# Experts in turn from the four groups, a further block's two halves in banks of their own, and bias products with 128 rows, in a hybrid backbone layer with a mixture of experts

## The chip, the cores and the metric

The kernel runs on one core of one Trainium2 chip. The metric is device time in microseconds (us), from the start of the program to its end, so lower is better. Before the change the median of 3 runs is 3455.18 us (3452.33 to 3460.63).

## What is computed

The reference is one layer: a token mix in two branches (a bidirectional recurrence with a matrix state per head, and a gated linear recurrence with a convolution), then a routed mixture of experts, each with a residual and a layer norm. Sizes: 1024 latent tokens, 256 context tokens, width 1024. Two pieces matter here. The first gives the recurrence its decays and its in-context rates, through low-rank ("lora") products of rank 64 with a bias, for both directions:

```python
w_log = -softplus(-(w0[:, None, None, :] + einsum('blr,erd->ebld', tanh(wd), w2))) - 0.5
decay = exp(-exp(w_log))
a = sigmoid(a0[:, None, None, :] + einsum('blr,erd->ebld', ad, a2))
```

The second is the mixture. There are 32 experts in 4 groups of 8. A token takes the best group, and in it the best two experts; an expert computes, for its tokens,

```python
(silu(xb @ w1[e]) * (xb @ w3[e])) @ w2[e]       # 1024 -> 512 -> 1024
```

## The kernel before, in words

The work goes through four parts one after the other: the input products and the linear recurrence (to some 940 us of the profile), the bidirectional recurrence (`phase_b`, to some 2340 us), the output products and the router (to some 2650 us), and the experts (`phase_d`, to some 3380 us), with a last layer norm behind them.

**The recurrence.** `phase_b` walks over 40 steps (4 pairs of heads' tiles, 10 pieces of 128 tokens), and for each over both directions `e`. The order of its instructions on every engine is written by a scheduler when the program is built, from generators that yield estimated delays; nobody wrote it by hand, so a small edit can move many rows. `stage_e` (L746) makes the decays and rates of one step and direction: four tiles of 128x128 in one PSUM bank, and for each of them four products that add up: three with 128 rows (L769 to L771, weights and inputs split into high and low bf16 parts) and one (L772) that adds the bias: its weights `T.b` are the bias in three bf16 parts, so 3 rows, and its moving operand is `ones3`, 3 rows of ones. ScalarE then takes the bank (L774). `T.b` is loaded once for each pair of tiles (L738), into a tile of 3 partitions.

**The experts.** `feed_weights` loads the weights: `todo` (L1283) lists, for each expert in the order of its number, 4 tiles of `e_w13` and 2 of `e_w2`, each of 1 MB; 16 such tiles fit on the chip. `ahead` (L1292) issues the next loads on SP's queue as tiles are given back. The tokens of an expert are gathered by an indirect DMA (`gather`), and transposed by TensorE (`x_t`).

Every expert has a first block of 64 tokens: `first` (L1688) computes its hidden values by `up` (L1619: 8 x 2 products of 512 columns, two half-height outputs side by side), `gate` (L1627) is silu on ScalarE and a multiplication on VectorE, `turn` (L1631) transposes on TensorE and copies on VectorE, `down` (L1638) multiplies with `e_w2`, and `put` (L1646) scales on VectorE and scatters the rows to memory from GpSimd. The loop at L1699 runs them interleaved: `first` of expert e+1, then `turn`, `x_t` and `down` around expert e. An expert with more than 64 tokens needs further blocks: `further` (L1671) loads the count into a register on every engine and branches; inside, `ffn` (L1658) is one further block. Up to three stand in nested branches. `ffn` has one PSUM bank `phb` for both halves of the hidden values (256 columns each), and runs them in turn:

```python
up(e, x, ph, A0)
gate(h, ph, A0)
up(e, x, ph, A1)
gate(h, ph, A1)
turn(hT, h, A0)
down(e, py, hT, A0)
turn(hT, h, A1)
down(e, py, hT, A1)
put(py, ap)
```

In `phase_d` the order on every engine is the order of the code (`manual_schedule`). PSUM there is full: two banks `ph` for the first blocks, one `phb`, one `pht`, two `py`, two for `x_t`. The counts of this input are such that 18 further blocks run: 11 in experts 8 to 15, 7 in experts 16 to 23, and none in experts 0 to 7 and 24 to 31.

## Time and profile before

| | |
|---|---|
| median of 3 runs | 3455.18 us (3452.33 to 3460.63) |
| the profiled execution, its own time | 3447.87 us |
| its span, first to last instruction | 3446.1 us |
| TensorE (PE) busy | 3091.9 us, 90% |
| VectorE (DVE) busy | 2162.2 us, 63% |
| ScalarE (ACT) busy | 1516.7 us, 44% |
| GpSimd (POOL) busy | 1231.1 us, 36% |
| mean granted TensorE clock | 0.921 of 2.4 GHz |

A row of the timeline gives the start, the duration, the engine, the line, output and inputs, the shapes and the count of merged instructions, and in brackets the idle time of the engine before it and what ended that. Matmuls overlap each other, and their ends are modelled: what a product costs in a stream is the distance from its start to the start of the next. A float32 product stands as two records.

### The profile page before, as it was taken

What the parts mean: (1) busy time and instruction counts of PE and PEld (TensorE: products, weight loads), DVE (VectorE), ACT (ScalarE), POOL (GpSimd) and SP (SyncE); (2) the same over time, 40 slices, a digit from 0 to 9 for tenths busy, and PEclk for the clock granted to TensorE, in tenths of its full rate; (3) what the DMA queues carried; (4) which work ended last, traced back from release to release, by engine and by line L of the source; (5) the groups of instructions that cost most, each with busy time, mean ns of one, the idle gap of its engine ahead of it and who ended that gap; (6) DMA issues with size and microseconds to landing.
All of it is one profiled execution on the core that took longest, in us unless ns stands there. A gap on an engine that the chain in (4) does not pass through costs nothing. (4 is left out here: it accounts for less than half of the span.)

```text
span 3446.1 us, 67028 instructions
## 1 busy us (share of the span) xinstructions
PE 3091.9 (90%) x26407; PEld 2288.7 (66%) x26407; DVE 2162.2 (63%) x4153; ACT 1516.7 (44%) x3127; POOL 1231.1 (36%) x1517
## 2 busy tenths in 40 slices
PE   7999998999999999999999999998886888988881
PEld 4877776777777878788878887886674333434330
DVE  6768998966638877987777878776585111111115
ACT  4466555667426666666566657653210000000003
POOL 1022322344325544755554557432042111111114
PEclk9999999999986999999878989999997999999996
DMA  5433345432532111311221123106426976484895
GB/s 207 136 109 107 128 140 187 140 98 80 174 132 60 55 57 52 98 51 58 66 78 46 54 65 95 39 16 202 153 93 253 407 280 254 168 321 177 336 380 213
DMA packets 265476, 496.80 MB, mean 144 GB/s; under 512 B 34690, under 2 KB 188002, under 8 KB 239484
## 3 DMA queue, kind: packets, MB, share of 16 engines
q1 hardware_dynamic: 243804, 443.16, 36.7%
q0 software_dynamic: 21280, 48.28, 3.8%
q8 instruction: 263, 4.31, 0.5%
q14 instruction: 129, 1.06, 0.1%
HBM read 437.37 MB, written 83.83 MB: 151 GB/s over the span
## 5 line engine op out<-in xcount | busy, mean ns | idle before, releaser
L234 PE MATMUL zl<-h_hi,wlo 128*128 128x512 f32 x944 | 326.5, 400 | 17.5 <-DVE wlo L157 17.5
L230 PE MATMUL zl<-h_hi,whi 128*128 128x512 f32 x944 | 325.7, 401 | 3.9 <-ACT acc L408 3.0
L232 PE MATMUL zl<-h_lo,whi 128*128 128x512 f32 x944 | 326.4, 400 | 0.6 <-DVE rstd L287 0.5
L1624 PE MATMUL ph<-r,xT 128*64 128x512 f32 x1024 | 254.1, 652 | 65.5 <-PEq L1674 33.7
L1649 POOL DMA_INDIRECT scr_yx<-yo,sidx x50 | 50.8, 1017 | 554.4 <-DVE yo L1648 235.5
L1613 ACT ACTIVATE xT<-pxt 128x512 f32<-128x512 f32 x37 | 22.1, 597 | 500.0 <-DVE hT L1636 423.4
L1624 PEld LDWEIGHTS ph<-r,xT 128*64 128x64 f32 x1024 | 90.6, 149 | 227.2 <-issue 224.8
L234 PEld LDWEIGHTS zl<-h_hi,wlo 128*128 128x128 f32 x944 | 179.6, 191 | 55.1 <-DVE wlo L157 20.0
L836 PE MATMUL pg<-qr,bk 64*128 64x128 f32 (+1 forms) x1280 | 211.3, 309 | 4.8 <-DVE bk L797 2.5
L230 PEld LDWEIGHTS zl<-h_hi,whi 128*128 128x128 f32 x944 | 179.6, 191 | 43.5 <-ACT acc L408 3.7
L232 PEld LDWEIGHTS zl<-h_lo,whi 128*128 128x128 f32 x944 | 180.4, 191 | 38.0 <-issue 1.4
L1636 DVE COPY hT<-pht 128x256 f32<-128x256 f32 x32 | 13.6, 425 | 299.0 <-PE pht L1635 299.0
L841 POOL TENSOR_TENSOR r<-st,hm 64x256 f32<-64x256 f32 x160 | 117.7, 736 | 212.7 <-ACT hm L840 208.9
L836 PEld LDWEIGHTS pg<-qr,bk 64*128 64x128 f32 x1280 | 176.6, 209 | 18.4 <-issue 4.8
L411 DVE SCALAR_TENSOR_TENSOR acc<-zt,drv,acc 128x960 f32<-128x960 f32 (+3 forms) x142 | 170.8, 1209 | 9.5 <-ACT acc L408 5.9
L1002 POOL TENSOR_TENSOR sp<-rv,pc 64x128 f32<-64x128 f32 x304 | 132.5, 454 | 93.7 <-DVE rv L1025 81.7
L893 PE MATMUL pu<-u,n 128*128 128x64 bf16 x2240 | 155.8, 200 | 3.8 <-DVE n L903 2.6
L157 DVE TENSOR_TENSOR wlo<-wraw,whi 128x1024 fp32r<-128x1024 f32 x67 | 101.1, 1509 | 86.9 <-ACT whi L156 83.1
L915 ACT ACTIVATE u<-pu 128x256 bf16<-128x256 f32 x280 | 106.0, 381 | 93.5 <-PE pu L893 89.5
L1624 PE MATMUL phb<-r,xT 128*64 128x256 f32 x1152 | 131.6, 381 | 14.2 <-DVE hb L1629 12.7
L893 PEld LDWEIGHTS <-n 128*128 128x128 bf16 x2240 | 124.0, 102 | 27.6 <-issue 7.8
L917 DVE TENSOR_TENSOR u<-pu,u 128x256 bf16<-128x256 f32 x280 | 115.7, 417 | 41.8 <-PE pu L893 38.1
(456 smaller groups left out, 8429.0 us busy)
## 6 DMA issues: line engine op xcount, KB each, us to landing
r<-in_e_w_dram SPq DMA_DIRECT2D x192, 1024.0 KB
wraw<-in_w_in_dram SPq DMA_DIRECT2D x59, 512.0 KB
adr<-in_w_ada_dram SPq DMA_DIRECT2D x32, 512.0 KB
zk<-scr_zk SPq DMA_DIRECT2D x80, 128.0 KB
kk<-scr_kk SPq DMA_DIRECT2D x80, 128.0 KB
lp<-scr_lp SPq DMA_DIRECT2D x80, 128.0 KB
v<-scr_zv SPq DMA_DIRECT2D x80, 128.0 KB
wada<-in_w_ada_dram SPq DMA_DIRECT2D x8, 1024.0 KB
```

Of the source, the lines that this page charges most:

```text
L157: nc.vector.tensor_sub(lo, raw, hi.bitcast(F32))
L230: nc.tensor.matmul(pz, z.hi[:, k], h_hi[:, k, t0:t0 + n], start=(k == 0), stop=False)
L232: nc.tensor.matmul(pz, z.hi[:, k], h_lo[:, k, t0:t0 + n], start=False, stop=False)
L234: nc.tensor.matmul(pz, z.lo[:, k], h_hi[:, k, t0:t0 + n], start=False, stop=(k == KT - 1))
L411: nc.vector.scalar_tensor_tensor(o, i, mures[:n, r, j:j + 1], o, op0=OP.mult, op1=OP.add)
L836: nc.tensor.matmul(pg[:, j, cols], G.bk[sr, e, j, 64 * h:64 * h + 128], G.qr[sr, e, j, cols], start=True, stop=True)
L841: G_.tensor_tensor(r[sr], w[sr], hm[sr], op=OP.subtract)
L893: nc.tensor.matmul(pt[:, j], l[:, j], r_ if len(r_.shape) == 2 else r_[:, j], start=first, stop=True, **kw)
L915: A_.activation(u, pt, AF.Copy)
L917: V.tensor_tensor(u, pt, u8, op=OP.add)
L1002: G_.tensor_tensor(sp[sr, e], G.rv[sr, h, e, :, i], pcs[:, e, :, k:k + 1].to_broadcast([64, 2, C]), op=OP.mult)
L1624: nc.tensor.matmul(ph[HALF[h]].rearrange("p a b c -> p (a b c)")[:, c], x[:, k], w13(e, k)[:, h, c], start=(k == 0), stop=(k == KT - 1))
```

## The change

1. **Bias products.** `ones3` and the bias weights become tiles of 128 rows, zeros but for the first three; the bias tile `lb` is one tile for the whole part, and each pair's load writes its first three rows.
2. **Experts' order.** `ORDER` takes one expert of each of the four groups in turn: 0, 8, 16, 24, 1, 9, ... Loads, gathers and the loop follow it; `q` is the place in the order, `e` the expert.
3. **Further blocks.** `ffn` takes two banks `pa` and `pb` from the ring `ph` that the first blocks use, `pht` gets a second bank, and `up` and `down` can run in pieces, with the transposes between the pieces.

```diff
-    ones3 = pk.tile([3, P], BF16, name="ones3")
-    V.tensor_scalar(ones3, ident[0:3], 0.0, 1.0, op0=OP.mult, op1=OP.add)
+    ones3 = pk.tile([P, P], BF16, name="ones3")
+    V.memset(ones3, 0.0)
+    V.tensor_scalar(ones3[0:3], ident[0:3], 0.0, 1.0, op0=OP.mult, op1=OP.add)
+    lb = pk.tile([P, 2, 2, 2, P], BF16, name="lb")
+    V.memset(lb, 0.0)
...
-        T.b = pe.tile([3, 2, 2, 2, P], BF16, name=f"b{pr}", tag="b")
-        nc.sync.dma_start(T.b.rearrange("p e i a c -> p e i (a c)"),
+        T.b = lb
+        nc.sync.dma_start(lb[0:3].rearrange("p e i a c -> p e i (a c)"),
...
-    todo = [(e, i) for e in range(NE) for i in range(6)]
+    todo = [(e, i) for e in ORDER for i in range(6)]
...
+ORDER = [8 * g + i for i in range(8) for g in range(4)]
...
-        pt = psx.tile([P, 2, P], F32, name="pht", tag="pht")
+        pt = psx.tile([P, 2, P], F32, name="pht", tag="pht", bufs=2)
...
-    acc_h = lambda nm: psx.tile([P, 2, 2, P], F32, name=nm, tag=nm, bufs=2 if nm == "ph" else 1)
+    acc_h = lambda: psx.tile([P, 2, 2, P], F32, name="ph", tag="ph", bufs=2)
...
-        ph, py, h, hT = acc_h("phb"), acc_y(), hidden("hb"), hidden("hbT")
-        up(e, x, ph, A0)
-        gate(h, ph, A0)
-        up(e, x, ph, A1)
-        gate(h, ph, A1)
+        pa, pb, py, h, hT = acc_h(), acc_h(), acc_y(), hidden("hb"), hidden("hbT")
+        up(e, x, pa, A0)
+        gate(h, pa, A0)
+        up(e, x, pb, A1, range(4))
         turn(hT, h, A0)
-        down(e, py, hT, A0)
+        up(e, x, pb, A1, range(4, KT))
+        gate(h, pb, A1)
+        down(e, py, hT, A0, (0,))
         turn(hT, h, A1)
+        down(e, py, hT, A0, (1,))
         down(e, py, hT, A1)
         put(py, ap)
...
-        for e in range(NE):
-            if e + 3 < NE:
-                gather(xgs[0][(e + 3) % 2], gidx[:, 0, e + 3:e + 4])
...
+        for q, e in enumerate(ORDER):
+            fetch(0, q + 3)
+            fetch(1, q + 2)
```

What moves on TensorE in a further block, first before (the rows of one `ffn`, behind the branch of L1674; `r_0` to `r_3` are the `e_w13` tiles, `r_4` and `r_5` the `e_w2` tiles):

```order
L1674 COMPARE_AND_BRANCH
L1624 MATMUL phb<-r_0_34562,xT 64x256 x4
L1624 MATMUL phb<-r_1_34564,xT 64x256 x4
L1624 MATMUL phb<-r_2_34566,xT 64x256 x4
L1624 MATMUL phb<-r_3_34568,xT 64x256 x4
...
L1635 MATMUL pht<-ident,hb 128x128
L1644 MATMUL py<-r_4_34570,hbT 64x512 x4
L1635 MATMUL pht<-ident,hb 128x128
L1644 MATMUL py<-r_5_34572,hbT 64x512 x4
```

and of the changed kernel, from the second half of the hidden values on (its lines are up to 7 higher: the branch is L1681, `up` L1628, `turn` L1639, `down` L1648):

```order
L1628 MATMUL ph<-r_0_34561,xT 64x256 x4
L1628 MATMUL ph<-r_1_34563,xT 64x256 x4
L1639 MATMUL pht<-ident,hb 128x128
L1628 MATMUL ph<-r_2_34565,xT 64x256 x4
L1628 MATMUL ph<-r_3_34567,xT 64x256 x4
L1648 MATMUL py<-r_4_34569,hbT 64x512 x2
L1639 MATMUL pht<-ident,hb 128x128
L1648 MATMUL py<-r_4_34569,hbT 64x512 x2
L1648 MATMUL py<-r_5_34571,hbT 64x512 x4
```

Before, both transposes stood behind all products of the hidden values and directly ahead of the products that need them. Now the first stands in the middle of the second half's products, and the second between two parts of the first half's `down`.

On VectorE the same block had the two multiplications of `gate`, then the two copies of `turn`; now they alternate:

```order
L1633 TENSOR_TENSOR hb<-ph,hb 128x128
L1640 COPY hbT<-pht 128x128
L1633 TENSOR_TENSOR hb<-ph,hb 128x128
L1640 COPY hbT<-pht 128x128
L1652 TENSOR_TENSOR yo<-py,gt_33547 128x512
```

In the recurrence the kinds and numbers of instructions on each engine stay the same but for two memsets on VectorE, and the order of TensorE's rows is the same for the first 193 of them behind the last output product; from there on the scheduler has written another order on every engine, with local exchanges throughout. The first place on TensorE, before and now:

```order
L769 MATMUL pl<-lp,w_6652 128x128
L770 MATMUL pl<-lp,w_6652 128x128
L771 MATMUL pl<-lp,w_6652 128x128
L772 MATMUL pl<-ones_6584,b_6654 128x128
L836 MATMUL pg<-qr_7302,bk_6656 128x64 x4
```

```order
L772 MATMUL pl<-lp,w_6655 128x128
L773 MATMUL pl<-lp,w_6655 128x128
L774 MATMUL pl<-lp,w_6655 128x128
L775 MATMUL pl<-ones_6584,lb 128x128
L839 MATMUL pg<-qr_7304,bk_6658 128x64 x4
```

The group of four stands as it stood; its bias product reads `lb` in place of `b`.

## Rows read from the trace of the kernel before

**Rows 1.** Windows of the recurrence and of a run of light experts.

```profile
core 0: us, PE busy (x) PEld busy (x) DVE busy (x) ACT busy (x) POOL busy (x), PEclk, DMA share, GB/s
1000.00:2300.00 1300.00, 1263.01 (x16894) 1054.28 (x16894) 1032.25 (x2671) 813.53 (x2193) 717.71 (x1120) 0.89 0.21 61
2700.00:2800.00 100.00, 80.78 (x354) 31.22 (x352) 12.84 (x24) 5.23 (x12) 18.29 (x18) 0.91 1.01 408
```

**Rows 2.** Timeline of PE in the recurrence at the full clock.

```profile
1507.20 0.23 PE L769 MATMUL pl<-lp,w 128*128 128x128 bf16 x1
1507.27 0.22 PE L770 MATMUL pl<-lp,w 128*128 128x128 bf16 x1
1507.32 0.22 PE L771 MATMUL pl<-lp,w 128*128 128x128 bf16 x1
1507.47 0.22 PE L772 MATMUL pl<-ones,b 3*128 3x128 bf16 x1
1507.63 0.23 PE L769 MATMUL pl<-lp,w 128*128 128x128 bf16 x1
```

**Rows 3.** Timeline of PE at half the clock.

```profile
1016.96 0.29 PE L769 MATMUL pl<-lp,w 128*128 128x128 bf16 x1
...
1017.61 1.96 PE L836 MATMUL pg<-qr,bk 64*128 64x64 f32 x8
```

**Rows 4.** Lines L771 and L772: duration ns min/median/max, first and last start.

```profile
L771 PE MATMUL pl<-lp,w x320: 216/219/314, 938.0 to 2254.8; 128*128 128x128 bf16 x160
L772 PE MATMUL pl<-ones,b x320: 224/224/284, 945.5 to 2255.0; 3*128 3x128 bf16 x160
```

**Rows 5.** Windows where the recurrence begins; columns as in group 1.

```profile
1012.80:1016.10 3.30, 2.55 (x25) 1.55 (x24) 1.82 (x3) 1.31 (x3) 2.38 (x6) 1.00 0.16 50
1016.10:1019.50 3.40, 3.40 (x19) 2.54 (x17) 0.86 (x2) 1.75 (x5) 2.66 (x6) 0.50 0.87 273
```

**Rows 6.** Waits of PE in the recurrence: us in total, times, longest.

```profile
PE pu L911 <- DVE u L917: 4.4, 5, 2.0
```

**Rows 7.** Timeline of PE, one further block.

```profile
2935.67 3.67 PE L1624 MATMUL phb<-r,xT 128*64 128x256 f32 x32 [0.70 <-DVE hb L1629]
2939.27 0.33 PE L1635 MATMUL pht<-ident,hb 128*128 128x128 f32 x1
2940.24 1.94 PE L1644 MATMUL py<-r,hbT 128*64 128x512 f32 x8 [0.64 <-DVE hbT L1636]
2942.82 1.94 PE L1644 MATMUL py<-r,hbT 128*64 128x512 f32 x8 [0.38 <-DVE hbT L1636]
```

**Rows 8.** Waits of PE among the experts.

```profile
PE py L1644 <- DVE hbT L1636: 18.5, 36, 0.6
PE phb L1624 <- DVE hb L1629: 12.7, 18, 0.7
```

**Rows 9.** Timeline of POOL: the scatters that begin and end a run.

```profile
2677.82 1.02 POOL L1649 DMA_INDIRECT scr_yx<-yo,sidx  x1 [10.98 <-DVEq L1674]
2808.27 1.03 POOL L1649 DMA_INDIRECT scr_yx<-yo,sidx  x1 [10.94 <-DVE yo L1648]
```

**Rows 10.** Timeline of PE, experts without further blocks.

```profile
2679.46 7.09 PE L1624 MATMUL ph<-r,xT 128*64 128x512 f32 x32 [2.67 <-PEq L1674]
2687.72 3.65 PE L1644 MATMUL py<-r,hT 128*64 128x512 f32 x16
2694.51 8.78 PE L1624 MATMUL ph<-r,xT 128*64 128x512 f32 x32 [3.13 <-PEq L1674]
...
2891.36 7.09 PE L1624 MATMUL ph<-r,xT 128*64 128x512 f32 x32 [2.22 <-PEq L1674]
...
3358.65 7.09 PE L1624 MATMUL ph<-r,xT 128*64 128x512 f32 x32 [0.48 <-PEq L1674]
```

**Rows 11.** Line L1674, the branch, on two engines: duration ns min/median/max.

```profile
L1674 PEldq COMPARE_BRANCH  x32: 70/5562/6924, 2661.1 to 3367.1; - x32
L1674 DVEq COMPARE_BRANCH  x32: 43/56/72, 2666.8 to 3370.7; - x32
```

More of the change, by code (lines that the diff above doesn't have):

```diff
@@ L1617, in w13, with up @@
         return RAW[e, k // 2].rearrange("p (k h c) -> p k h c", k=2, h=2)[:, k % 2]
-    def up(e, x, ph, parts):
+    def up(e, x, ph, parts, ks=range(KT)):
         c = slice(256 * parts.start, 256 * parts.stop)
-        for k in range(KT):
+        for k in ks:
             for h in range(2):
@@ L1636, in turn, with down @@
         V.tensor_copy(hT[:, parts], pt[:, parts])
-    def down(e, py, hT, parts):
+    def down(e, py, hT, parts, hs=range(2)):
         for i in range(parts.start, parts.stop):
             w = RAW[e, 4 + i].rearrange("p (h d c) -> p h d c", h=2, d=2)
-            for h in range(2):
+            for h in hs:
                 for d in range(2):
@@ L1654, in phase_d, with further @@
     hidden = lambda nm: bp.tile([P, 2, P], F32, name=nm, tag=nm, bufs=2)
-    acc_h = lambda nm: psx.tile([P, 2, 2, P], F32, name=nm, tag=nm, bufs=2 if nm == "ph" else 1)
+    acc_h = lambda: psx.tile([P, 2, 2, P], F32, name="ph", tag="ph", bufs=2)
     acc_y = lambda: psx.tile([P, 512], F32, name="py", tag="py", bufs=2)
     def ffn(e, x, ap):
-        ph, py, h, hT = acc_h("phb"), acc_y(), hidden("hb"), hidden("hbT")
-        up(e, x, ph, A0)
-        gate(h, ph, A0)
-        up(e, x, ph, A1)
-        gate(h, ph, A1)
+        pa, pb, py, h, hT = acc_h(), acc_h(), acc_y(), hidden("hb"), hidden("hbT")
+        up(e, x, pa, A0)
+        gate(h, pa, A0)
+        up(e, x, pb, A1, range(4))
         turn(hT, h, A0)
-        down(e, py, hT, A0)
+        up(e, x, pb, A1, range(4, KT))
+        gate(h, pb, A1)
+        down(e, py, hT, A0, (0,))
         turn(hT, h, A1)
+        down(e, py, hT, A0, (1,))
         down(e, py, hT, A1)
         put(py, ap)
-    def further(e, xT):
+    def further(q, xT):
+        e = ORDER[q]
         n = count(cnt[0:1, e:e + 1])
@@ L1676, in further @@
             with tc.If(n > 128):
-                x2 = x_t(xgs[1][e % 2], "xT2")
+                x2 = x_t(xgs[1][q % 2], "xT2")
                 ffn(e, x2[:, :, HALF[0]], sidx[:, 2, e:e + 1])
@@ L1680, in further, with fetch, first @@
                     ffn(e, x2[:, :, HALF[1]], sidx[:, 3, e:e + 1])
-    for e in range(2):
+    def fetch(b, q):
+        if q < NE:
+            gather(xgs[b][q % 2], gidx[:, b, ORDER[q]:ORDER[q] + 1])
+    for q in range(2):
         for b in range(2):
-            gather(xgs[b][e], gidx[:, b, e:e + 1])
+            fetch(b, q)
     with tc.manual_schedule():
         X, HID = {}, {}
-        def first(e):
-            HID[e] = acc_h("ph"), hidden("h")
-            up(e, X[e][:, :, HALF[0]], HID[e][0], AB)
+        def first(q):
+            HID[q] = acc_h(), hidden("h")
+            up(ORDER[q], X[q][:, :, HALF[0]], HID[q][0], AB)
         X[0] = x_t(xgs[0][0], "xT")
-        gather(xgs[0][0], gidx[:, 0, 2:3])
+        fetch(0, 2)
         first(0)
@@ L1698, in phase_d @@
         ahead(4)
-        for e in range(NE):
-            if e + 3 < NE:
-                gather(xgs[0][(e + 3) % 2], gidx[:, 0, e + 3:e + 4])
-            if e + 2 < NE:
-                gather(xgs[1][e % 2], gidx[:, 1, e + 2:e + 3])
-            if e + 1 < NE:
-                first(e + 1)
-            h, hT, py = HID[e][1], hidden("hT"), acc_y()
+        for q, e in enumerate(ORDER):
+            fetch(0, q + 3)
+            fetch(1, q + 2)
+            if q + 1 < NE:
+                first(q + 1)
+            h, hT, py = HID[q][1], hidden("hT"), acc_y()
             turn(hT, h, AB)
-            if e + 2 < NE:
-                X[e + 2] = x_t(xgs[0][e % 2], "xT")
-            if e + 1 < NE:
-                gate(HID[e + 1][1], HID[e + 1][0], AB)
+            if q + 2 < NE:
+                X[q + 2] = x_t(xgs[0][q % 2], "xT")
+            if q + 1 < NE:
+                gate(HID[q + 1][1], HID[q + 1][0], AB)
             down(e, py, hT, AB)
@@ L1714, in phase_d @@
             ahead(2)
-            if e + 1 < NE:
-                further(e + 1, X[e + 1])
+            if q + 1 < NE:
+                further(q + 1, X[q + 1])
                 ahead(4)
@@ L1742, in phase_d @@
             tt(po, S.io[:, None, :].to_broadcast([P, 16, P]), pb[:, :, None].to_broadcast([P, 16, P]), op=OP.is_equal)
-            px = psx.tile([P, 2, NE], F32, name="pxall", tag="pht")
+            px = psx.tile([P, 2, NE], F32, name="pxall", tag="pxt1")
             for j in range(16):
```

## The prediction, made blind

> **What bounds the kernel now.** I read the page first, for the busy shares, then windows over the two parts that the change touches, then the timeline of TensorE (PE) and its waits in each, because an average over the whole span says nothing on either part. In the recurrence [rows 1] PE is busy for 1263 of 1300 us, VectorE for 1032 (79%), and the longest group of PE's own waits is 4.4 us in all [rows 6]: this part is as long as PE's list of products, and what shortens the list shortens it. Matmuls overlap there, so the price of a product is the distance between starts, not its duration. The mean granted clock is 0.89. PE has two levels, 1.2 and 2.4 GHz, so about 2 x 0.11 x 1300 = 286 us of the part run at half the clock.
>
> Among the experts there are two different stretches. With further blocks, PE works without a pause except inside each block [rows 7]. Where experts have none ("light" ones: 0 to 8 and 22 to 31, with 11, 15 and 16), the DMA engines are full (share 1.01, 408 GB/s [rows 1]) and PE waits for 2.2 to 3.2 us ahead of the next expert's first product [rows 10]. The trace names PE's own sequencer at the branch of `further`, not a load. That branch takes PE 5.56 us in the median, while VectorE passes the same one in 0.056 us [rows 11]. A light expert takes 16.3 us: scatters of experts 0 and 8 start at 2677.82 and 2808.27 [rows 9], and 130.45 / 8 = 16.3.
>
> **The change, part by part.** The sum is made against the profiled execution's own 3447.87 us (span 3446.1). The median of the runs is 3455.18, 7.3 us more, so the forecast is put on the median.
>
> **Bias products.** In [rows 2] the 128-row products follow each other by 0.07 and 0.05 us, but the 3-row product starts 0.15 us behind its predecessor, and the next 128-row product 0.16 us behind it. With 128 rows it should stand in the stream like the others: 0.15 - 0.05 and 0.16 - 0.07 are 0.19 us, and 320 such products [rows 4] make 61 us of PE's time. The group of four takes 0.43 us now (1507.20 to 1507.63) and should take about 0.24. No row shows the saving on the part's length. The lower bound is 0: VectorE would be at 1032 of 1239 us, 83%, and could become what PE waits for. The upper bound adds the clock. A group takes 0.65 us at half the clock [rows 3], against 0.43, so each us at half loses 1 - 0.43 / 0.65 = 0.34 us, and 286 us lose 97. Where the part begins, the granted clock is 1.00 while PE runs almost nothing but these groups, with 2.55 us busy in 3.30, and 0.50 right behind them [rows 5]. If full rows kept a third of such stretches at 2.4 GHz, 32 us more would go: 93. A loss is possible too, since the scheduler writes another order; that is a rival below. I take 45, three quarters of 61, nearest to the row of PE's waits: they are so small that most of PE's saving should arrive, but a new order and a shorter list will uncover some waits. VectorE's two memsets and the once-allocated bias tile cost nothing: they run while output products fill PE, and the loads of the next pair wait for the last reader as before. If that cover were gone, it would be a fraction of a us, once.
>
> The Trainium skill has a rule against this term: "TensorE: Matmul & The Clock Gate", section "Why this matters for your kernels", says that one product with 32 rows takes the same time as one with 128. By it the 45 would be 0. Our durations agree with it (224 against 219 ns [rows 4]), the starts do not (0.15 and 0.16 against 0.05 and 0.07 us [rows 2]). The skill's "TensorEngine Tiling (Array Packing)", section "Key Properties", says that a change of tiling mode drains the engine, which fits the starts.
>
> **Further blocks.** In [rows 7] PE stands idle three times a block: 0.70 us ahead of the second half's products, which wait for `gate` of the first half since both write one bank; 0.64 us for the first copy of the transposed half; and 0.38 us for the second copy. That is 1.72 us, and 18 blocks make 31; the groups of waits say the same, 18.5 + 12.7 = 31.2 [rows 8]. In the new order each wait has cover. The second half's products go to another bank and start at once. `gate` of the first half (0.70) and the copy behind the first transpose (0.33 + 0.64) each lie beside half of those products, 3.67 / 2 = 1.83 us. `gate` of the second half (0.70) and the second copy (0.33 + 0.38) each lie beside a quarter of `down`, 1.94 / 2 = 0.97. The thinnest cover is 0.97 against 0.71; if the last one failed, 18 x 0.38 = 7 would come back. Bounds 24 and 31; I take 31, since every wait has its row and every cover is longer.
>
> The shared ring `ph` adds one wait: the first product of the next expert now needs ScalarE and VectorE to have passed the branch of the expert before, too, or its `gate` inside. Behind it on PE stands the whole next expert. In a light expert, VectorE is done when the scatter starts, 2677.82 [rows 9], and PE's product starts at 2679.46 [rows 10], so 1.6 us hide it, and this costs 0. Only where PE's own branch is short (0.48 us at 3358.65 [rows 10]) could a few tenths show, a few times: under 2 us, left at 0.
>
> **Order of the experts.** The runs of light experts are broken up: five at the start (0, 8, 16, 24, 1), at most three between heavy ones, six at the end. It is tempting to count the whole idle time of those runs as waiting for weights. But PE's own work in a light expert is 11.91 us (2679.46 to 2687.72 + 3.65), and the wait at the branch is 2.22 us at 2891.36 too [rows 10], right behind heavy experts where the loads had caught up. So 14.1 us remain, and 15.8 when the clock drops in the gap (products 8.78 instead of 7.09 us). In the mean that is 15.0, against 16.3: 1.3 us at best for each expert that leaves a run. Six light experts now come first behind a heavy one, three did before, and second ones gain in part: I take 7 us. Bounds are 0 (every light expert still pays branch and clock) and 15 x 1.3 = 20. The gathers and loads only change their order; POOL and SP issue as many as before.
>
> The Trainium skill speaks against a larger term: "Runtime: NRT & Kernel Launch", section "Instruction fetch mechanics", says that a taken branch whose target is not in the window forces a fetch of the target page before anything runs. By it this wait belongs to the branch, no order of the experts removes it, and the 7 would be near 0; the long branch on PE alone [rows 11] fits.
>
> Sum: 45 + 31 + 7 = 83. That gives 3447.87 - 83 = 3365 for an execution like the profiled one, and 3455 - 83 = **3372 us** for the median.
>
> **The rivals.**
>
> *PE's saving in the recurrence is given back.* The 3-row product costs the stream what any product costs, or VectorE and ScalarE take over. Against it stand the starts in [rows 2]; for it VectorE's 79%. Then 31 + 7 = 38 remain: 3417.
>
> *More than the forecast.* All 61 arrive, the clock keeps 32, the light experts give 20: 61 + 32 + 31 + 20 = 144, so 3311. [Rows 5] speak for the clock, but other groups of products also stand ahead of half-clock stretches, and the recurrence's waits are not zero.
>
> *Slower: the clock in the recurrence.* The new order there puts short products and waits together so that the clock is granted less. Place: 1000 to 2300 us. Price: 0.34 us for each us more at half. It eats the whole gain from 83 / 0.34 = 244 us more at half, a granted mean of 0.80 in place of 0.89. At 0.75 it would be 364 us more and 124 us lost: 3496. For it: such a stretch at 0.50 exists where waits and few products coincide [rows 5]. Against it: the same products are there, and what leaves them is idle time between starts.
>
> *The change doesn't do what it says* in the blocks: if the shared ring made `pa` or `pb` wait for a bank, the 31 would go and 3403 remain; the order of the rows gives each bank's last reader long before its next writer, so I leave this inside the forecast's range.
>
> **How the numbers follow.** Forecast 0.70, with a range of its own of 3335 to 3405; saving given back 0.13; more 0.10; clock 0.05; other 0.02. The range 3320 to 3420 takes in the forecast, nearly all of the first rival and a part of the second; below it I leave some 0.07, above it some 0.08. A difference of 0.2%, about 7 us, is what a measurement of this kernel can tell from none. Faster 0.91 (forecast, first and second rival, less a little for their edges), same 0.03, slower 0.06.
>
> **What would show it.** Right: the bias product starts 0.05 to 0.07 us behind its predecessor; the stretch between the first and the last group of four is shorter by about 45 us, at a granted clock of 0.89 or more; a further block has no bracketed wait on VectorE and takes 1.7 us less; PE's waits at the branch are still 2 to 3 us, some 20 times; DMA shares of 1.01 become rare. Wrong: starts of 0.15 us that stay (first rival); starts that shrink and a part that does not, with PE waiting for VectorE; a granted mean under 0.85 (third rival); or a wait of `ph` for VectorE ahead of an expert's first product.

## The result, and the profile after

The changed kernel takes 3418.95 us in the median of 20 runs (3389.43 to 3449.67), the kernel before 3457.20 in 20 runs beside it (3443.14 to 3497.36). The ratio is 0.9869, with a 95% interval of 0.984 to 0.9898: between 35 and 55 us faster. The profiled execution took 3421.91 us, with a span of 3420.1 and a mean granted clock of 0.913. The gain was forecast as 83 us and is about half of that. The forecast time of 3372 is missed by 47 us; 3418.95 lies inside the range by 1 us, less than the measurement can tell.

The window of the recurrence of [rows 1], now, and the whole recurrence, from the first `pl` to the last `pgf`, of the kernel before and then of this one:

```profile
core 0: us, PE busy (x) PEld busy (x) DVE busy (x) ACT busy (x) POOL busy (x), PEclk, DMA share, GB/s
1000.00:2300.00 1300.00, 1224.67 (x16798) 1063.03 (x16797) 1043.53 (x2656) 811.85 (x2186) 724.19 (x1116) 0.87 0.21 62
...
937.90:2340.50 1402.60, 1360.26 (x17801) 1134.82 (x17801) 1077.16 (x2761) 845.40 (x2262) 733.39 (x1144) 0.90 0.22 65
...
943.10:2342.50 1399.40, 1318.34 (x17736) 1141.30 (x17736) 1090.81 (x2753) 845.09 (x2260) 737.75 (x1140) 0.88 0.22 65
```

PE is busy for 38 us less of the same 1300 us, and the granted clock is lower. Over the whole recurrence PE is busy for 42 us less, and idle for 81.1 us where it was idle for 42.3. The line of its last products, L893 before, begins its last `pgf` at 2340.5 in the profile before and at 2342.5 now; from the first `pl` it is 1402.6 us before (937.9 to 2340.5) and 1399.4 now (943.1 to 2342.5).

```profile
L896 PE MATMUL pgf<-u,ux x320: 190/193/261, 1092.9 to 2342.5; 128*128 128x64 bf16 x160
...
L772 PE MATMUL pl<-lp,w x320: 216/219/314, 943.1 to 2263.6; 128*128 128x128 bf16 x160
L775 PE MATMUL pl<-ones,lb x320: 216/219/314, 952.8 to 2263.7; 128*128 128x128 bf16 x160
```

The bias product itself is as forecast. PE's timeline, to set beside [rows 2]:

```profile
1509.26 0.23 PE L772 MATMUL pl<-lp,w 128*128 128x128 bf16 x1
...
1509.39 0.22 PE L774 MATMUL pl<-lp,w 128*128 128x128 bf16 x1
1509.44 0.22 PE L775 MATMUL pl<-ones,lb 128*128 128x128 bf16 x1
1509.50 0.22 PE L772 MATMUL pl<-lp,w 128*128 128x128 bf16 x1
```

The product with 128 rows starts 0.05 us behind its predecessor, and the next one 0.06 us behind it; a group of four takes 0.24 us in place of 0.43. This group is a dense one: over all bias products at the full clock (248 and 260 of the 320 lie wholly in it) the two distances sum to 0.31 us before and 0.14 now in the mean, and 0.17 x 320 = 55 us. PE's waits in the recurrence (us in total, times, longest), from 1020 to 2250 us, first of this kernel and then of the kernel before:

```profile
PE pu L914 <- DVE u L920: 8.4, 11, 2.0
PE ps L896 <- DVE midx L936: 8.0, 15, 1.8
PE ph L880 <- DVE x L882: 7.9, 8, 2.4
PE pt L896 <- DVE ux L852: 7.0, 14, 1.2
```

```profile
PE pu L911 <- DVE u L917: 4.4, 5, 2.0
PE ph L877 <- DVE x L879: 4.3, 4, 2.4
...
PE ps L893 <- DVE midx L933: 2.1, 3, 1.5
PE pt L893 <- DVE ux L849: 1.7, 5, 0.6
```

Every one of these groups is longer now, by a factor of 1.8 to 4, and all four wait for VectorE. Over the whole recurrence PE's waits for VectorE sum to 61 us, before to 31.

A further block, to set beside [rows 7]:

```profile
2759.16 5.40 PE L1628 MATMUL ph<-r,xT 128*64 128x256 f32 x48 [0.30 <-ACT xT L1617]
2764.49 0.33 PE L1639 MATMUL pht<-ident,hb 128*128 128x128 f32 x1
2764.75 1.95 PE L1628 MATMUL ph<-r,xT 128*64 128x256 f32 x16
2766.53 1.03 PE L1648 MATMUL py<-r,hbT 128*64 128x512 f32 x4
2767.49 0.33 PE L1639 MATMUL pht<-ident,hb 128*128 128x128 f32 x1
2767.75 2.79 PE L1648 MATMUL py<-r,hbT 128*64 128x512 f32 x12
```

Inside the block no row has a bracket: PE does not wait. From scatter to scatter the first and third further block of an expert take 11.16 us, 13.25 before. Light experts, ahead of which PE waits at the branch [rows 10], are no faster (their 21 distances sum to 336 us, before to 324), and the place where a new wait shows first is ahead of the second expert in the order. Its products before, and then those of this kernel, with a later light expert's:

```profile
2664.88 7.09 PE L1624 MATMUL ph<-r,xT 128*64 128x512 f32 x32 [0.59 <-PEq L1674]
```

```profile
2668.64 8.78 PE L1628 MATMUL ph<-r,xT 128*64 128x512 f32 x32 [3.44 <-DVEq L1681]
...
2716.32 8.78 PE L1628 MATMUL ph<-r,xT 128*64 128x512 f32 x32 [3.37 <-PEq L1681]
```

Before, that second expert's product waited 0.59 us, for PE's own branch. Now it waits 3.44 us for VectorE to have passed the branch (DVEq), which VectorE does at 2668.1, behind `gate` of the first expert. The shared ring is the reason: the same 3.44 us stand in `further_alone` below, which has the ring, and no such wait in `order_alone`, which has not. PE's waits among the experts, from 2650 to 3420 us:

```profile
PE ph L1628 <- PEq L1681: 33.9, 11, 4.1
PE ph L1628 <- DMA r<-in_e_w_dram: 20.2, 6, 3.5
...
PE ph L1628 <- DVEq L1681: 6.6, 4, 3.4
...
PE ph L1628 <- DVEq L1683: 4.2, 4, 1.0
PE ph L1628 <- DVEq L1686: 2.1, 2, 1.0
```

The groups of [rows 8], 18.5 and 12.7 us, are gone. From the first scatter to the last it is 699.6 us before and 671.4 now (2683.27 to 3354.71), 28 less.

The ratios leave out runs that took over 1.5% more than their kernel's fastest, which the medians keep, and the profiles of `order_alone`, `bias_alone` and `short_skip` below are of such runs, at a lower granted clock, so their recurrence is read only with the clock's part taken out.

### The profile page after: what moved, and what is told of

Same layout as the page of the kernel before. It is cut to its first block, busy times and chain, and to the rows that moved or that the text cites. A ratio compares the mean times of both kernels' runs of the same rounds, so it can differ in the third digit from the quotient of the medians.

```text
span 3420.1 us, 66973 instructions
## 1 busy us (share of the span) xinstructions
PE 3051.5 (89%) x26407; PEld 2298.8 (67%) x26407; DVE 2179.7 (64%) x4155; ACT 1517.5 (44%) x3127; POOL 1238.7 (36%) x1517
## 5 line engine op out<-in xcount | busy, mean ns | idle before, releaser
L1628 PE MATMUL ph<-r,xT 128*64 128x256 f32 (+1 forms) x2176 | 387.3, 509 | 76.9 <-PEq L1681 33.9
L1628 PEld LDWEIGHTS ph<-r,xT 128*64 128x64 f32 x2176 | 170.5, 142 | 288.2 <-issue 246.4
L157 DVE TENSOR_TENSOR wlo<-wraw,whi 128x1024 fp32r<-128x1024 f32 x67 | 101.2, 1510 | 84.9 <-ACT whi L156 81.1
L783 POOL TENSOR_SCALAR km<-cb,ka 128x128 f32<-128x128 f32 x160 | 97.9, 621 | 83.1 <-ACT cb L777 81.5
```

The costliest lines, as they stand in the source:

```text
L157: nc.vector.tensor_sub(lo, raw, hi.bitcast(F32))
L1628: nc.tensor.matmul(ph[HALF[h]].rearrange("p a b c -> p (a b c)")[:, c], x[:, k], w13(e, k)[:, h, c], start=(k == 0), stop=(k == KT - 1))
```

## The experiments

Every kernel ran beside the kernel before on the same chip. That kernel's median was 3476.40 us beside `order_alone`, `further_alone`, `bias_alone` and `old_order`, 3470.88 beside `changed_again`, `three_rows`, `old_order_18_tiles` and `old_order_no_branch`, and 3468.06 beside the other four. A ratio is good to some 0.4% either way, about 13 us.

### One part of the change at a time

`order_alone` is the kernel before with `ORDER`, and the loads, gathers and loop that follow it:

```diff
+ORDER = [8 * g + i for i in range(8) for g in range(4)]
-    todo = [(e, i) for e in range(NE) for i in range(6)]
+    todo = [(e, i) for e in ORDER for i in range(6)]
...
-        for e in range(NE):
+        for q, e in enumerate(ORDER):
```

Expected: 

> The kernel before with the new order of the experts alone (loads, gathers and loop by ORDER; bias products and further blocks as before). Theory on record: each light expert that leaves a run of light ones gains up to 1.3 us, 7 us in all, so about 7 us faster than before. Rival, from the trace of the changed kernel, where the 21 intervals of light experts sum to 336 us against 324 before: every light expert still pays the branch, and one that follows several heavy ones waits for weights, since a heavy expert holds its six tiles to its last block. Then 0 to 12 us slower, all of it between the first and the last scatter.

Measured: median 3474.83 against 3476.40; ratio 0.995 (0.9908 to 0.9993). From the first scatter to the last 698.6 us, before 699.6. So the order is worth 1 us in its own stretch, and the medians are 1.6 us apart. The ratio says more, 17 us (2 to 32); the recurrence has the same instructions in the same order as before, nothing in the experts' stretch accounts for it, and its cause is not shown. In that stretch the 21 distances of light experts sum to 2.9 us less, and the first blocks of the others to 3.3 us more. PE's waits ahead of first products, of the kernel before and then of this one:

```profile
PE ph L1624 <- PEq L1674: 33.7, 13, 3.4
PE ph L1624 <- DMA r<-in_e_w_dram: 24.8, 8, 4.0
...
PE ph L1624 <- PEq L1676: 5.8, 5, 2.2
```

```profile
PE ph L1625 <- PEq L1676: 52.2, 20, 3.8
...
PE ph L1625 <- PEq L1678: 9.6, 5, 2.4
PE ph L1625 <- DMA r<-in_e_w_dram: 3.3, 1, 3.3
```

Waits put down to weights go from 24.8 us to 3.3, and those at the branch from 39.5 us to 61.8; the sum is 64.3 before and 65.1 after. The names mislead here. In the kernel before, all eight products whose wait is put down to weights start 0.31 or 0.32 us behind the end of PE's branch, and the others behind this branch start 0.31 to 0.36 us behind it. So the branch held the eight as well, and the weights cost them nothing.

`further_alone` is the kernel before with the new `ffn` and its banks (the third part of the diff shown above).

Expected: 

> The kernel before with the new further block alone (two banks of the shared ring, transposes amid the products; the order of the experts and the recurrence as before). Theory on record: 31 us faster (18 blocks by 1.72). From the trace of the changed kernel: 18 blocks by 2.08 are 37, less five waits of the first products for a bank of the shared ring at about 0.5 to 1 us, so 32 to 36 us faster. Rival: the blocks' gain is taken back because weights come no faster; then under 15 us. The recurrence should be as long as before within 5 us.

Measured: median 3444.14 against 3476.40, 32 us less; ratio 0.9935 (0.9896 to 0.9974), 23 us less (9 to 36). From the first scatter to the last 672.9 us, 27 less than before; the recurrence, whose code is that of before, takes 1395.0 us. The 18 blocks give 18 x 2.09 = 38. What is missing lies mostly at two places: from the last scatter of expert 10 to that of 11 it is 21.90 us (14.32 before), and from the last of 14 to that of 15 22.52 (16.25 before), 14 us together. PE's timeline at the first of them, and windows there:

```profile
2877.56 2.76 PE L1625 MATMUL ph<-r,xT 128*64 128x512 f32 x11 [3.50 <-PEq L1678]
2883.36 7.77 PE L1625 MATMUL ph<-r,xT 128*64 128x512 f32 x21 [3.04 <-issue]
```

```profile
2880.00:2890.00 10.00, 6.96 (x19) 2.66 (x19) 0.00 (x0) 0.00 (x0) 1.00 (x1) 0.66 1.02 419
...
2910.00:2920.00 10.00, 10.00 (x74) 5.10 (x72) 1.29 (x5) 0.56 (x2) 0.00 (x0) 1.00 0.04 14
```

These are the first products of expert 12. PE stops behind the 11th of 32 records for 3.04 us, while the DMA engines are full (1.02), and half the clock follows (0.66 in this window). It looks like a wait for weights, but the profile names none ("issue"), and the next products need no further tile. What the trace does show is a packet of 16 KB on a queue of instructions (q8) that lands 1.47 us before PE goes on. At the second place PE stops for 4.83 us in the same way, and such a packet lands 1.50 us before the end. So PE waits for its own code there; the experiments on the branch below show the same packets. In the further blocks of expert 12, which hold its tiles, the DMA engines then stand idle (0.04). So loads cannot run on through the blocks of a heavy expert, and fall together with the code of the light ones. The theory's 32 to 36 are near the medians' 32, but what takes back is the code more than the ring; the rival's 15 falls by the medians and the stretch, though the ratio's interval (9 to 36) reaches below it.

`bias_alone` is the kernel before with the bias products of 128 rows (the first part of the diff); the recurrence has the changed kernel's order on every engine.

Expected: 

> The kernel before with the bias products of 128 rows alone; the scheduler writes the recurrence's rows in the same order as for the changed kernel. Theory on record: 45 us faster. Rival (saving given back as waits and lower clock, as the trace of the changed kernel looks): within 15 us of before, with the stretch from the first to the last group of four as long as before and PE less busy in it.

Measured: median 3458.45 against 3476.40, 18 us less; ratio 0.9943 (0.9907 to 0.9979), which is 20 us less (7 to 32). Its recurrence takes 1441.4 us at a granted clock of 0.83. It is a gain, but less than half of the 45 on record, and a little more than the rival's 15. So the rows are worth something, and the size had to be found elsewhere.

The three parts are -1 and -27 (stretches) and -20 (ratio): 48 us, against 38 (medians) to 45 (ratio) for the whole. By the ratios alone they are -17, -23 and -20, 60 us. Each is good to some 13 us, so whether the parts add up is not shown.

### What a product with 128 rows is worth, and what the order is worth

`three_rows` has the bias product on the first three rows of the changed kernel's tiles; `three_rows_other_order` and `full_rows_other_order` have the two memsets on GpSimd, with 3 and with 128 rows. They were meant as three further orders of the recurrence. In the traces `three_rows` and `full_rows_other_order` have orders of their own, but the recurrence of `three_rows_other_order` has the order of the kernel before: PE's, VectorE's and ScalarE's instructions from the first `pl` to the last `pgf` are the same, one by one. So there are two orders with 3 rows and two with 128. `changed_again` is the changed kernel once more.

```diff
-nc.tensor.matmul(pl[:, i, a], T.b[:, e, i, a], ones3, ...)
+nc.tensor.matmul(pl[:, i, a], T.b[0:3, e, i, a], ones3[0:3], ...)
```

```diff
-    V.memset(ones3, 0.0)
+    nc.gpsimd.memset(ones3, 0.0)
...
-    V.memset(lb, 0.0)
+    nc.gpsimd.memset(lb, 0.0)
```

Expected, `changed_again`: 

> The changed kernel itself, on the chip of this call, as the value to compare the others with. Some 35 to 45 us faster than before.

Expected, `three_rows`: 

> The changed kernel with the bias product on the first three rows of the same tiles (result the same); the scheduler writes a third order of the recurrence. It tells what full rows are worth where all else of the change stays. Theory on record: 45 us slower than the changed kernel. Theory now (of the 61 us that leave PE's list some 20 reach the end, the rest turns into waits of PE for VectorE): about 20 us slower. Rival (the rows are worth nothing, and what bias_alone gained was luck of its order): within 8 us of the changed kernel. In the recurrence, with the clock's part taken out at 0.34 us for each us at half, the same three numbers.

Expected, `three_rows_other_order`: 

> Three-row bias products in one more order (that of three_rows with the memsets on GpSimd). before, three_rows and this are then three orders with 3 rows, to set beside two orders with 128. If full rows are worth about 60 in the mean, the 3-row orders lie 20 to 75 us behind the changed kernel, this one anywhere between. If the order is the larger part, this one comes out as fast as the changed kernel.

Expected, `full_rows_other_order`: 

> The changed kernel with the two memsets of the bias tiles on GpSimd in place of VectorE: the same products with 128 rows, but the scheduler writes another order of the recurrence. Theory (PE's freed time meets VectorE, whatever the order): within 10 us of the changed kernel, about 40 to 45 us faster than before. Rival (the order written decides, by some 40 us either way, as the slow three_rows hints): over 15 us away from the changed kernel.

Measured. The length of the recurrence is from the first `pl` to the last `pgf<-u,ux`; from it is taken 0.34 us for each us at half the clock, as on record, that is 0.34 x 2 x (1 - clock) x 1300 (an estimate, to some 5 us, since the clock stands with two digits); a letter names an order:

| kernel | rows | order | median, us | ratio to before | recurrence, us | clock | at full clock, us |
|---|---|---|---|---|---|---|---|
| before | 3 | A | | 1 | 1402.6 | 0.89 | 1305 |
| further_alone | 3 | A | 3444.14 | 0.9935 | 1395.0 | 0.90 | 1307 |
| three_rows | 3 | C | 3494.57 | 1.0074 (1.004 to 1.0108) | 1475.3 | 0.83 | 1325 |
| three_rows_other_order | 3 | A | 3449.01 | 0.9959 (0.9914 to 1.0004) | 1424.0 | 0.87 | 1309 |
| bias_alone | 128 | B | 3458.45 | 0.9943 | 1441.4 | 0.83 | 1291 |
| changed kernel | 128 | B | 3418.95 | 0.9869 | 1399.4 | 0.87 | 1284 |
| changed_again | 128 | B | 3421.63 | 0.9883 (0.9841 to 0.9926) | 1389.2 | 0.88 | 1283 |
| full_rows_other_order | 128 | D | 3428.89 | 0.9883 (0.9819 to 0.9947) | 1393.3 | 0.88 | 1287 |

(The first value of the changed kernel is that of its own comparison, above.) `before`, `further_alone` and `bias_alone` have nothing else of the change than the name says; the others have all of it but the rows.

Windows of the recurrence, of `changed_again`, `full_rows_other_order`, `three_rows_other_order` and `three_rows`; the columns are those of the first window above:

```profile
1000.00:2300.00 1300.00, 1220.91 (x16983) 1059.73 (x16982) 1055.52 (x2684) 815.44 (x2198) 728.07 (x1120) 0.88 0.21 61
```

```profile
1000.00:2300.00 1300.00, 1231.11 (x16858) 1068.23 (x16857) 1038.32 (x2664) 813.89 (x2189) 730.25 (x1120) 0.88 0.21 61
```

```profile
1000.00:2300.00 1300.00, 1262.04 (x16506) 1052.77 (x16505) 1013.89 (x2616) 799.17 (x2157) 709.73 (x1107) 0.87 0.21 61
```

```profile
1000.00:2300.00 1300.00, 1253.55 (x15743) 1041.11 (x15741) 981.49 (x2505) 768.50 (x2062) 682.80 (x1060) 0.83 0.21 60
```

What follows. With 3 rows PE is busy for 1254 to 1263 of 1300 us, with 128 rows for 1221 to 1231, in two orders each. At the full clock the two orders with 128 rows lie at 1283 to 1291 us, order A with 3 rows at 1305 to 1309 in three kernels, and order C at 1325: full rows are worth some 20 us against A and 40 against C. The two kernels with the memsets on GpSimd say the same: 3449.01 against 3428.89 us, run side by side. An order with 128 rows that is as slow as A, or one with 3 that is as fast as B, was not met, but four orders are few. The theory said 20 for `three_rows`, and 73 us came (3494.57 against 3421.63): about 42 of it stand in the table at the full clock, and the rest goes with the clock, 0.83 against 0.88. Order C is slow by itself, and in all its runs: their granted clock over the whole kernel is 0.90 in the mean, 0.91 in the kernel before beside them. `three_rows_other_order` did not test what was expected of it, a third order. So one kernel with another order is no price for an instruction. `full_rows_other_order` came within 7 us of the changed kernel, as the theory had it: another order with full rows ends at the same length.

The freed time can be followed in PE's idle time. From the first `pl` to the last `pgf` PE idles for 42 to 46 us in order A (`before`, `further_alone`, `three_rows_other_order`), for 76 to 83 us in order B (`bias_alone`, the changed kernel, `changed_again`) and for 71 us in order D. So of the 55 to 61 us that the starts of the bias products gave back, 39 stand in the changed kernel as waits, and 16 to 22 are left, in accord with the table. The expectation of `full_rows_other_order`, that PE's freed time meets VectorE whatever the order, held in this second order too: PE's waits for VectorE are 52 us there, 31 before.

### What bounds the light experts

`old_order` is the changed kernel with the experts in the order of their numbers, `old_order_18_tiles` that with 18 tiles for the weights (18 fit as well, not only the 16 that the kernel before has):

```diff
-ORDER = [8 * g + i for i in range(8) for g in range(4)]
+ORDER = list(range(32))
...
-NRAW = 16
+NRAW = 18
```

Expected, `old_order`: 

> The changed kernel with the experts in the order of their numbers again (new bias products and new further blocks stay). If the new order costs 12 us, this is 12 us faster than the changed kernel, about 48 us faster than before (ratio 0.986 or less); if it gains 7 us as on record, this is 7 us slower than the changed kernel, about 31 to 38 us faster than before.

Expected, `old_order_18_tiles`: 

> The changed kernel with the experts in the order of their numbers and 18 tiles for the weights in place of 16. Theory: faster blocks leave the loads behind; in old_order PE waits 19.2 us for weights (6 times), and two tiles are 2 MB, some 5 us of loading ahead. Then the waits for weights shrink to under 8 us and the kernel is some 8 to 14 us faster than old_order, about 50 us faster than before. Rival: the branch takes the place of each wait for weights, as it does in order_alone; then within 5 us of old_order.

Measured: `old_order` 3435.10 against 3476.40, ratio 0.9906 (0.9872 to 0.994); 673.8 us from the first scatter to the last, against 671.4 of the changed kernel. That the new order costs 12 us falls. Its 7 us are not in the stretch, where it gains 2.4; the runs can't tell (41 us less than before by the medians, 33 by the ratio, where 31 to 38 were expected with the 7). `old_order_18_tiles` 3441.73 against 3470.88, ratio 0.9919 (0.9887 to 0.9952); 671.0 us from the first scatter to the last. Of PE's waits, first of `old_order`, then with 18 tiles:

```profile
PE ph L1628 <- PEq L1681: 37.2, 12, 3.9
PE ph L1628 <- DMA r<-in_e_w_dram: 19.2, 6, 3.5
```

```profile
PE ph L1628 <- PEq L1681: 51.2, 17, 3.5
...
PE ph L1628 <- DMA r<-in_e_w_dram: 3.3, 1, 3.3
```

As in `order_alone`: 19.2 us put down to weights become 3.3, and the branch rises from 37.2 to 51.2. The rival was right that nothing is gained; but the branch did not take the place of weights, it had held these products before: in `old_order` the six that are put down to weights start 0.42 to 0.47 us behind its end, the others 0.42 to 0.49.

Three kernels take away the branch or part of it. In `old_order_no_branch` and `no_branch` the count and the branch are left out for the experts that need no further block with this input; they are 22 (the expectations say 21, which is the number of distances between scatters). In `short_skip` these experts keep the first branch, but the second and third blocks behind it are left out. For another input such kernels would leave out blocks.

```diff
+LIGHT = set(range(9)) | {11, 15, 16} | set(range(22, 32))
...
+        if e in LIGHT:
+            return
         n = count(cnt[0:1, e:e + 1])
         with tc.If(n > 64):
             ffn(e, xT[:, :, HALF[1]], sidx[:, 1, e:e + 1])
```

```diff
         with tc.If(n > 64):
             ffn(e, xT[:, :, HALF[1]], sidx[:, 1, e:e + 1])
+            if e in LIGHT:
+                return
             with tc.If(n > 128):
```

Expected, `old_order_no_branch`: 

> The changed kernel with the experts in the order of their numbers, and the count and branch left out for the 21 experts that have no further block in this input (a kernel for this input alone; the output is the same). Theory (branch): PE's waits at the branch, some 50 us in all, and the lower clock behind them go, 50 us or more faster than old_order. Rival (weights): a light expert's 6 MB still take 15.4 us to load at 408 GB/s, so a run of light experts goes from 16.8 to 15.4 us each, about 20 us faster, and PE's waits there are for weights instead.

Expected, `no_branch`: 

> The changed kernel, with the new order, and the count and branch left out for the 21 experts without further blocks in this input (for this input alone). Theory: in order_alone the branch took the place of the waits for weights (24.8 us of them before, 3.3 there). Without the branch the new order can pay: in old_order_no_branch PE still waits 34 us for weights in the runs of light experts. Then 10 to 25 us faster than old_order_no_branch, so 95 to 125 us faster than before. Rival (weights come no faster in the mean, heavy experts hold their tiles): within 8 us of old_order_no_branch.

Expected, `short_skip`: 

> The changed kernel with the branch kept for the light experts, but with one further block behind it in place of three nested ones, so that the skip is a third as long (enough for this input). If the price hangs on the length that is skipped, the waits at the branch (some 45 us for PE) shrink by half or more, 20 us or more faster than the changed kernel. If every skip of a block costs the same, within 8 us of the changed kernel.

Measured:

| kernel | median, us | ratio to before | first scatter to last, us | a light expert |
|---|---|---|---|---|
| changed kernel | 3418.95 | 0.9869 | 671.4 | mostly 14.2 to 17.8 |
| old_order_no_branch | 3368.84 | 0.9728 (0.9677 to 0.9778) | 618.1 | 11.69, late in a run 15.2 to 18.1 |
| short_skip | 3363.78 | 0.9698 (0.9639 to 0.9757) | 612.8 | 12.96 |
| no_branch | 3333.04 | 0.9621 (0.9558 to 0.9684) | 584.0 | 11.69 |

The last column is the distance from scatter to scatter. PE's timeline at a light expert's first products, in `short_skip` and then in `no_branch`; then a group of PE's waits among the experts of `short_skip`, and one of `old_order_no_branch`:

```profile
2731.44 7.09 PE L1629 MATMUL ph<-r,xT 128*64 128x512 f32 x32 [1.05 <-DVEq L1682]
```

```profile
2705.33 7.04 PE L1629 MATMUL ph<-r,xT 128*64 128x512 f32 x32
```

```profile
PE ph L1629 <- DVEq L1682: 24.9, 21, 3.4
```

```profile
PE ph L1629 <- DMA r<-in_e_w_dram: 34.3, 31, 4.4
```

The branch, of the changed kernel and then of `short_skip`: duration ns min/median/max:

```profile
L1681 PEldq COMPARE_BRANCH  x32: 70/5198/6913, 2662.1 to 3341.3; - x32
```

```profile
L1682 PEldq COMPARE_BRANCH  x32: 70/220/375, 2684.0 to 3304.3; - x32
```

What follows. The branch bounds the light experts, in either order. Without it the old order gains 56 us between its scatters (673.8 to 618.1), and by the medians 61 (102 us less than before, against 41), more than the 50 expected; then weights hold it, and PE waits 31 times for them, so both theories name a part. The new order without the branch is another 34 us shorter there, 584.0 against 618.1, where 10 to 25 were expected; it is the fastest kernel of all, 135 us less than before. So the order is worth 34 us once nothing stands in front of it, and 1 to 2 as long as the branch does. And the price of the branch hangs on what is skipped: with one block behind it in place of three, PE's branch goes from 5198 to 220 ns in the median, and the kernel takes 104 us less than before, some 60 less than the changed kernel. The next in line is the wait for VectorE that the shared ring brought, 24.9 us in 21 times, 1.2 us for each light expert: 12.96 - 11.69 = 1.27.

The trace also shows what the long skip waits for. In each of its 22 times in the changed kernel a packet of 16 KB on a queue of instructions lands 1.3 to 1.5 us before the branch ends; in `short_skip` no such packet lands within a skip. Such packets go over the same DMA engines as the weights. One skip starts at 2709.72 us and takes 6.17, one at 2679.03 takes 3.65; the queue of instructions during the whole of the first (packets, MB, share), and the windows of the first 2.5 us of both, of the changed kernel:

```profile
q8 instruction: 1, 0.02, 1.1%
```

```profile
2679.03:2681.53 2.50, 2.50 (x14) 0.87 (x12) 0.69 (x2) 0.16 (x1) 0.00 (x0) 1.00 0.06 10
2709.72:2712.22 2.50, 2.50 (x14) 0.87 (x12) 0.70 (x2) 0.17 (x1) 0.00 (x0) 1.00 1.02 426
```

So it is in all 22: the five whose first 2.5 us find the DMA engines nearly idle (a share of 0.12 or less) take 3.4 to 3.8 us, the other 17 (0.64 or more) take 5.1 to 6.9. A long skip waits for code, and the loads of weights lengthen it.

## Why the prediction came out as it did

**The sign and the range held; two of three sizes did not.** Forecast were 45 + 31 + 7 = 83. Measured alone they are about 20, 27 and 1. All three were too large, and the range held by 1 us, with luck: `changed_again` came out at 3421.63, outside it.

**Bias products: 20 in place of 45.** The price of the product was right: starts of 0.05 and 0.06 us in a dense group, and some 55 us over all 320 products in place of the 61, since not every one has full-row neighbours. The step that failed is the next one: "they are so small that most of PE's saving should arrive", drawn from [rows 6]. A short list of waits says how long PE waits with the present list. It does not say how soon VectorE's results would have been there. Behind a wait of zero there may be no slack at all. PE's waits for VectorE doubled, from 31 to 61 us, and its idle time rose by 39. The lower bound, VectorE that "could become what PE waits for", was the better half, although VectorE is busy for only 80% of the window (1043.53 of 1300): this points to the chain from PE to VectorE and back and not to the busy share, though no run here makes VectorE's part of it shorter. The clock, taken as a possible gain of 32 us, gave nothing back: 0.87 and 0.88 in the two profiles against 0.89, and 0.91 over the whole kernel in the runs of `changed_again` as in those of the kernel before beside it. That the first rival, "PE's saving in the recurrence is given back", came to 3417 is only half a hit: about a third of the 61 us did arrive, and its number is so near because the other two terms came out smaller.

The Trainium skill, "TensorE: Matmul & The Clock Gate", section "Why this matters for your kernels", says that one product with 32 rows takes the time of one with 128; by it full rows would be worth 0. The durations agree (224 ns with 3 rows [rows 4], 219 with 128); the distances between starts do not, and they set the price in a dense stream.

**Further blocks: 27 in place of 31.** All three waits of [rows 7] went, and the blocks became 2.09 us shorter, not 1.72: 38 us in all. The 0.37 us beyond the three waits were not taken apart. Light experts took 10 us back in `further_alone` (their 21 distances sum to 334.9 us, before to 324.5): at the two places above, where loads and the code of a light expert meet, 14 us went, of which a part is saved elsewhere. The term had no place for this: it took what the blocks save as what the experts' stretch saves. And the shared ring has a price.

**The shared ring: not 0.** The step that failed is "in a light expert, VectorE is done when the scatter starts, ... so 1.6 us hide it". The 1.6 us are the length of PE's own branch, not a reserve of VectorE's. Where PE's branch is short, the chain shows: in `short_skip` PE's last product of a light expert ends at 2730.39, VectorE's multiplication with it takes from 2730.44 to 2731.13, VectorE signals that it has passed the branch at 2731.17, and PE starts at 2731.44 [1.05]. The prediction saw the place ("only where PE's own branch is short") and left it at 0. In the changed kernel the wait stands 10 times with 12.9 us (6.6 + 4.2 + 2.1), and a part of it only replaces the wait for PE's own branch: 3.44 us in place of 0.59 at the second expert, and 12.96 in place of 12.46 us from scatter to scatter at each of the six skips of a nested branch. That is some 6 us, an estimate (2.85 + 6 x 0.5). This was the last point of "what would show it wrong", and it came.

**Order: 1 in place of 7.** The reading of [rows 10] was right, that the branch and not the load holds light experts. The step that failed took 1.3 us "for each expert that leaves a run" all the same. The branch held all of them, those that the profile puts down to weights too, and an expert that leaves a run still pays it: `order_alone` has 64.3 and 65.1 us of these waits, and what light experts gain (2.9 us) the first blocks of the others lose (3.3). At 2891.36, where the prediction took the loads to have caught up, the DMA engines are full too (1.01 over the first 2.5 us of that branch). The sentence on the Trainium skill, "Runtime: NRT & Kernel Launch", section "Instruction fetch mechanics", had the better forecast, near 0. That section of the Trainium skill says that a taken branch forces a fetch if its target is not in the window at hand; 5198 ns for the long skip against 220 for the short one, and the packets of code behind every long one, agree with that.

**The signs.** Of those named for a right forecast, the starts, the blocks and the waits at the branch came (11 put down to the branch and the 6 put down to weights, up to 4.1 us); the recurrence that is 45 us shorter did not. Of those for a wrong one, two came: PE waits for VectorE, and `ph` does ahead of a first product.

**Slower through the clock** did not come in the changed kernel. But `three_rows` shows the mechanism at work in another order, with a granted clock of 0.83 and 1325 us at the full clock.

## What to carry to other kernels

An engine that is busy for 97% with hardly a wait need not be the only bound: before a shorter list is booked as shorter time, ask when the next operand would have been there. Where two waits end in the same place, the name that the profile gives can be the wrong one: compare how long behind each candidate the work starts, and add up both groups of waits before and after. An order that a scheduler writes can move by tens of microseconds from an edit that changes no work (`three_rows` and `three_rows_other_order` differ in the engine of two memsets, and by 46 us), or not move at all, so look at the order itself; a price needs several orders or a stretch at one clock. A branch that skips much code is worth shortening before anything around it is rearranged.

## What the runs showed of the hardware that was not expected

PE's skip over three further blocks takes 5198 ns in the median and over one 220 ns, and with the short skip the whole kernel goes to 0.9698 of the time before. The long one waits for 16 KB of code, which come over the DMA engines, so that it takes 3.4 to 3.8 us where these are idle and 5.1 to 6.9 where the loads of weights fill them. How the price rises between these two lengths was not tried, nor was a kernel with short skips that serves every input.

The same recurrence, instruction for instruction, runs at different mean granted clocks in different executions: 0.89 in `old_order`, with 1388.4 us from the first `pl` to the last `pgf`, and 0.85 in `old_order_18_tiles`, with 1423.8. The 35 us are what 0.34 us for each us at half the clock make of the 0.04: 0.34 x 2 x 0.04 x 1300 = 35. Stretches of the experts at half the clock mostly go with the long branch: from the first scatter to the last the granted clock is 0.96 in the changed kernel, and 0.99 in `short_skip` and `no_branch`. A light expert's first products take 8.78 us behind a wait of 3.37 us, and 7.04 where nothing stands before them.
